# Shared filter sum on ScalarE and GpSimd ahead of the filters, and memory preparation in three split passes, in a decoder trunk

## The chip, the cores and the metric

The kernel runs on one core of a Trainium2 chip. The time is the device time of one execution in microseconds; the profile is of one execution of its own. The core has five engines with a queue each: TensorE (PE; its weight loads are shown apart as PEld), VectorE (DVE), ScalarE (ACT), GpSimd (POOL) and SyncE (SP), which here issues the DMAs. An engine executes its queue in order. SBUF is the on-chip memory of 128 partitions, PSUM the eight banks that matmuls write.

## The reference

A trunk of two layers on x of 1024 tokens by 1024 channels, in float32. Layer 0 mixes tokens with a Conformer convolution, layer 1 with an attention that is not touched here. After the mixer each layer does cross-attention into 256 memory tokens (4 heads of 256) and an MLP with squared ReLU. What matters:

```python
def conformer_conv(h, w_pw1, b_pw1, w_dw, b_dw, ln_g, ln_b, w_pw2, b_pw2):
    u = h @ w_pw1 + b_pw1
    a, gate = jnp.split(u, 2, axis=-1)
    u = a * jax.nn.sigmoid(gate)
    u = lax.conv_general_dilated(u, w_dw[:, None, :], window_strides=(1,),
        padding=[(CONV_WIDTH - 1, 0)], dimension_numbers=("NWC", "WIO", "NWC"),
        feature_group_count=D_MODEL) + b_dw          # 31 taps, each channel for itself
    u = jax.nn.silu(layernorm(u, ln_g, ln_b))
    return u @ w_pw2 + b_pw2

def memory_cross_attention(h, mem_n, w_q, w_k, w_v, w_o):   # mem_n = rmsnorm(mem, norm_memsrc_g)
    q = (h @ w_q).reshape(B, S, MEM_HEADS, MEM_HEAD_DIM)
    k = (mem_n @ w_k).reshape(B, MEM_LEN, MEM_HEADS, MEM_HEAD_DIM)
    v = (mem_n @ w_v).reshape(B, MEM_LEN, MEM_HEADS, MEM_HEAD_DIM)
    s = jnp.einsum("bshd,bmhd->bhsm", q, k) / math.sqrt(MEM_HEAD_DIM)
    p = jax.nn.softmax(s, axis=-1)
    return jnp.einsum("bhsm,bmhd->bshd", p, v).reshape(B, S, D) @ w_o
```

## The kernel before

Channels lie on partitions: x is 8 chunks (NCH) of 128 channels, each in two tiles of 512 tokens (HALF). A float32 product is mostly done in three passes on operands that are split into a high part, rounded to the format float32r, and a low part, the rest: low by high, high by low, high by high (`passes`, L262; `product`, L266). The high part is a copy on ACT, the low part a subtraction on DVE (`split`, L150, and `low`, L147). When `passes` gets a single part on each side it issues one plain float32 matmul, which the profile shows as two records.

The stage of the change is the start: `conv_layer` (L293) with `memory_matrices` (L433) interleaved.

- `conv_layer` loads x, normalizes it into split operands and goes over the 8 chunks. `gated_unit` (L362) computes a chunk's gated value by 2 x 2 products of 8 x 3 passes, ACT's sigmoid (sg, L368) and a multiplication on DVE (u, L370). u holds even and odd tokens apart.
- `convolve` (L386) filters a chunk of 128 channels with 31 taps, all on DVE. It uses the identity that even and odd outputs share a sum over the odd tokens with taps added in pairs (`both`: one instruction, L396, and 15 of L400), to which each half adds a filter of differences: d0 with 16 taps for one half, d1 with 15 for the other (L408). Both halves accumulate in X. The instructions are put in order at compile time; in the trace the taps of the two halves alternate. Then each half is added into `acc` (L354) for the layer norm.
- After the last chunk come the layer norm (`layer_norm`: L310 to L318), then `linear` with the weights pw2, whose outputs L324 adds to x.
- `memory_matrices` is a generator that is advanced a step at a time: four steps a head (K, V, the product of wq with K, the product of V with wo), 4 heads, 2 layers, 32 steps. Four steps are asked for before the filters, two a chunk, and the rest after the last chunk. A step loads two weight tiles of 512 KB (`get`, three tiles) and multiplies in plain float32: 16 products of 256 columns for the first three kinds, 8 of 512 columns for the fourth. Results go to DRAM (mqk, mvo) through the evacuations L483 and L501 on ACT. `mem_attention` reads them afterwards.

PSUM has eight banks: here 4 for the preparation, 2 for the gated unit and pw2, 2 shared ones. Small tiles called "t" (norms, squares and the like) rotate through 4 buffers. `tc.high_priority` moves what it encloses ahead at compile time.

Of the kernel before, what the change touches and what calls it, by code (L numbers as in the profile page):

```python
# [19 lines left out]
P = 128  # L20
# [66 lines left out]
def trunk(ctx, tc, a, out):  # L87
# [98 lines left out]
    def add_squares(acc, ch):  # L186

        sq = nrm.tile([P, HALF], F32, name="sq", tag="t", bufs=4)
        act.activation(sq, ch, AF.Square)
        if acc is None:  # L190
            return sq
        dve.tensor_tensor(acc, acc, sq, op=ALU.add)
        return acc
# [99 lines left out]
    def conv_layer(pm, prep):  # L293
        with tc.tile_pool(name="conv", bufs=2) as cp:
# [43 lines left out]
            acc = [cp.tile([P, HALF], F32, name=f"acc{s}", bufs=1) for s in range(2)]  # L338
            for m in range(NCH):
                if m:  # L340
                    u = padded()
                    for sl in HALVES:
                        gated_unit(pm, cp, m, ahead, hs, u[:, :, PAD // 2 :], sl)
                if m + 1 < NCH:
                    ahead = gate_weights(m + 1)
                for _ in range(2):
                    next(prep, None)

                convolve(cp, m, u, pairs[:, m])
# [36 lines left out]
    def convolve(cp, m, u, sums):  # L386


        n, k = S // 2, TAPS // 2
        even, odd = u[:, 0, :], u[:, 1, :]  # L390
        d0 = cp.tile([P, n + k], F32, name="d0")
        d1 = cp.tile([P, n + k - 1], F32, name="d1")
        dve.tensor_tensor(d0, even[:, : n + k], odd[:, : n + k], op=ALU.subtract)
        dve.tensor_tensor(d1, even[:, 1 : n + k], odd[:, : n + k - 1], op=ALU.subtract)
        both = cp.tile([P, n], F32, name="both")
        dve.tensor_scalar(  # L396
            both, odd[:, :n], sums[:, 0:1], col("dw_b", m), op0=ALU.mult, op1=ALU.add
        )
        for j in range(1, k + 1):
            dve.scalar_tensor_tensor(  # L400
                both, odd[:, j : j + n], sums[:, j : j + 1], both, op0=ALU.mult, op1=ALU.add
            )
        out = [X[:, m, sl] for sl in HALVES]
        for s, d, taps in ((0, d0, k + 1), (1, d1, k)):
            y = both
            for j in range(taps):
                w = col("dw_w", m * TAPS + 2 * j + s)
                dve.scalar_tensor_tensor(  # L408
                    out[s], d[:, j : j + n], w, y, op0=ALU.mult, op1=ALU.add
                )  # L410
                y = out[s]
# [21 lines left out]
    def memory_matrices(pp, pq, layer):  # L433
# [4 lines left out]
        def get(src):  # L438
            raw = pp.tile([P, NCH, P], F32, name="praw", bufs=3)
            nc.sync.dma_start(raw, src)  # L440
            return raw

        mem = pp.tile([P, NCH, MEM], F32, name="mem", bufs=1)
        nc.sync.dma_start(mem, a["memT"])
        if layer == 0:
            r = inverse_rms([mem[:, c, :] for c in range(NCH)], RMS_EPS)
# [3 lines left out]
        for c in range(NCH):  # L450
            act.activation(mem[:, c, :], mem[:, c, :], AF.Copy, scale=col(f"src{layer}", c))
        for h in range(MEM_HEADS):
            kv = []
            for w, n in ((wk, "kt"), (wv, "vt")):
                t = bank(pq).rearrange("p (c m) -> p c m", c=2)
                for c in range(2):
                    x = get(w[2 * h + c])
                    product(t[:, c, :], [((x[:, k, :],), (mem[:, k, :],)) for k in range(NCH)])
                o = pp.tile([P, 2, MEM], F32, name=n, bufs=1)
                if w is wk:  # L460
# [4 lines left out]
                    with tc.high_priority(offset=SMALL_FIRST):  # L465
                        dve.tensor_tensor(o, t, rb, op=ALU.mult)
                else:
                    act.copy(o, t)
                kv.append(o)
                yield  # L470
            kt, vt = kv
            for j in range(2):

                x = get(wq[h, j])
                for g in range(2):
                    t = bank(pq).rearrange("p (f m) -> p f m", f=2)
                    o = pp.tile([P, 4, P], F32, name="o").rearrange("p (f b) n -> p f (b n)", f=2)
                    for f in range(2):
                        product(t[:, f, :], [
                            ((x[:, 4 * c + 2 * g + f, :],), (kt[:, c, :],)) for c in range(2)  # L480
# [7 lines left out]
            for j in range(2):  # L488

                x = get(wo[h, j])  # L490
                for mc in range(2):
# [3 lines left out]
                            (vt[:, c, mc * P : (mc + 1) * P],),  # L495
                            (x[:, 4 * c : 4 * c + 4, :].rearrange("p b n -> p (b n)"),),
# [866 lines left out]
    with prep_pools(4) as pools, banks(2) as pm:  # L1363
        conv_layer(pm, chain(*(memory_matrices(*pools, l) for l in range(2))))
# [81 lines left out]
```

## Time and profile before

| | us |
|---|---|
| median of 3 runs | 2822.05 (2818.59 to 2823.66) |
| profiled execution | 2825.31 |
| its span | 2823.3 |
| until the last output of pw2 begins | 525.5 |

| whole span | busy us | share |
|---|---|---|
| PE | 2740.8 | 97% |
| DVE | 2030.9 | 72% |
| ACT | 1278.3 | 45% |
| POOL | 703.1 | 25% |

The span runs from the first to the last instruction. Busy shares are averages over stages with different limits, so the stage of the change has to be read by itself. In rows of groups the last parts are: output and inputs by the program's names, shapes, count, then busy us and mean ns of one, then the idle time before them and what ended it. In rows of one line or tile, three durations stand as min/median/max in ns, with the first and the last start in us. In rows of the timeline and the chain the first two numbers are start and length in us. All 512-column float32r passes of the kernel overlap in the pipeline, so a record's length is more than its distance to the next.

### The profile page before, as it was taken

The numbers are of one execution on the slowest core, as the hardware profiler recorded it, in microseconds if no ns is written. First come the engines' busy times: TensorE is split into PE (matmuls) and PEld (weight loads), VectorE is DVE, ScalarE is ACT, GpSimd is POOL, SyncE is SP. The second block draws the span as 40 slices with busy tenths as digits, with TensorE's granted clock in tenths as the row PEclk, the third lists the DMA queues.
The fourth block names the chain that finished last, engine by engine and source line by source line (L and its number), as shares of the span: only waits on it lengthen the run. The fifth ranks groups of instructions, "written<-read, shape, count | busy, mean of one in ns | idle before, by whom it ended". The sixth has DMA issues, their size and how long they took to land.

```text
span 2823.3 us, 36214 instructions
## 1 busy us (share of the span) xinstructions
PE 2740.8 (97%) x12968; PEld 2261.3 (80%) x12968; DVE 2030.9 (72%) x3358; ACT 1278.3 (45%) x2293; POOL 703.1 (25%) x473
## 2 busy tenths in 40 slices
PE   8999999999999999999899999989999999989998
PEld 6777777888888877888688888878888788878886
DVE  5999984555776576777788888875546855577776
ACT  5212143433555553333466666673423655543332
POOL 0000000000065625774000000000000365525773
PEclk9999999999999999999899999999999999999999
DMA  6334364322165585652222221243213455655651
GB/s 219 120 119 135 114 206 124 101 90 70 65 230 177 178 309 187 227 199 89 69 68 70 57 65 55 69 136 98 94 64 105 149 176 190 218 208 197 227 201 61
DMA packets 165428, 390.68 MB, mean 138 GB/s; under 512 B 17264, under 2 KB 46192, under 8 KB 164992
## 3 DMA queue, kind: packets, MB, share of 16 engines
q1 hardware_dynamic: 165248, 388.37, 40.9%
q8 instruction: 102, 1.67, 0.2%
q14 instruction: 78, 0.64, 0.1%
HBM read 270.79 MB, written 113.31 MB: 136 GB/s over the span
## 4 chain that ended last, share of the span: by engine, by line
PE 74%; DVE 12%; ACT 5%; DMA 5%; issue 3%; POOL 1%; SPq 0%; DVEq 0%; POOLq 0%; ACTq 0%
PE mm L1070 34%; PE mm L269 29%; PE mm L1255 5%; DVE w L148 2%; DVE op L148 2%; DVE x L408 1%; PE mm L1341 1%; DVE x L1310 1%; DMA ua<-x 1%; ACT x L1315 1%; PE mm L1353 1%; PE mm L1354 1%; DVE both L400 1%; DVE wl L148 1%; ACT pth L151 1%
## 5 line engine op out<-in xcount | busy, mean ns | idle before, releaser
L1070 PE MATMUL mm<-op,w 128*128 128x512 f32 x5424 | 1242.4, 391 | 24.5 <-ACT m L955 8.7
L1070 PEld LDWEIGHTS mm<-op,w 128*128 128x128 f32 x5424 | 1020.5, 189 | 243.2 <-ACT m L955 9.6
L269 PE MATMUL mm<-op,wh 128*128 128x512 f32 x1056 | 330.5, 394 | 4.2 <-DVE op L148 4.2
L148 DVE TENSOR_TENSOR w<-r,w 128x512 fp32r<-128x512 f32 x264 | 262.6, 998 | 30.5 <-ACT w L653 30.5
L653 ACT CAST w<-r 128x512 fp32r<-128x512 f32 x264 | 163.3, 622 | 262.0 <-PE mm L1070 233.2
L269 PEld LDWEIGHTS mm<-op,wh 128*128 128x128 f32 x1056 | 200.2, 190 | 48.5 <-DVE op L148 6.5
L1255 PE MATMUL mm<-op,wh 128*128 128x512 f32 x736 | 231.4, 396 | 0.0
L148 DVE TENSOR_TENSOR w<-t,w 128x512 fp32r<-128x512 f32 x180 | 178.2, 1005 | 63.2 <-ACT w L653 63.1
L269 PE MATMUL mm<-op,wl 128*128 128x512 f32 x528 | 210.5, 400 | 7.1 <-DVE wl L148 6.2
L207 POOL TENSOR_TENSOR r<-v,mhalf 128x4 f32<-128x4 f32 (+1 forms) x15 | 16.8, 1117 | 741.0 <-DVE v L205 741.0
L647 POOL TENSOR_TENSOR t<-r,t 128x512 f32<-128x512 f32 x104 | 174.9, 1681 | 91.4 <-DVE w L148 54.2
L653 ACT CAST w<-t 128x512 fp32r<-128x512 f32 x180 | 112.0, 622 | 169.8 <-PE mm L1070 140.6
L151 ACT CAST wh<-raw 128x1024 fp32r<-128x1024 f32 x96 | 100.7, 1050 | 193.8 <-PE mm L269 97.5
L865 POOL TENSOR_TENSOR x<-x,x 128x512 f32<-128x512 f32 x112 | 160.2, 1455 | 112.6 <-ACT x L878 101.6
L967 DVE TENSOR_TENSOR x<-mm,x 128x512 f32<-128x512 f32 x160 | 109.5, 684 | 91.1 <-PE mm L1070 73.7
L1255 PEld LDWEIGHTS mm<-op,wh 128*128 128x128 f32 x736 | 139.2, 189 | 26.7
L269 PE MATMUL mm<-op,xsh 128*128 128x512 f32 x512 | 158.0, 393 | 0.0
L1255 PE MATMUL mm<-op,wl 128*128 128x512 f32 x368 | 155.0, 421 | 1.9 <-ACT q L1275 1.9
L151 ACT CAST pth<-mm 128x512 fp32r<-128x512 f32 (+1 forms) x224 | 105.9, 495 | 108.5 <-PE mm L556 80.8
L408 DVE SCALAR_TENSOR_TENSOR x<-d,par,x 128x512 f32<-128x512 f32 x232 | 154.5, 746 | 0.0
L647 POOL TENSOR_TENSOR t<-r,r 128x512 f32<-128x512 f32 x52 | 80.2, 1542 | 295.1 <-DMA r<-in_ff_w 191.0
L1315 ACT ACTIVATE x<-x,nb 128x128 f32<-128x128 f32 (+7 forms) x128 | 99.5, 778 | 109.3 <-DVE nb L1313 100.0
(188 smaller groups left out, 4689.6 us busy)
## 6 DMA issues: line engine op xcount, KB each, us to landing
r<-in_ff_w SPq DMA_DIRECT2D x128, 512.0 KB, 4.0
op<-ua SPq DMA_DIRECT2D x80, 512.0 KB, 6.8
us<-x SPq DMA_DIRECT2D x128, 256.0 KB, 2.9
op<-us SPq DMA_DIRECT2D x64, 512.0 KB, 5.6
raw<-mvo SPq DMA_DIRECT2D x32, 512.0 KB, 3.4
ua<-ul SPq DMA_DIRECT2D x64, 256.0 KB, 2.2
ua<-uh SPq DMA_DIRECT2D x60, 256.0 KB, 2.3
raw<-in_pw SPq DMA_DIRECT2D x24, 512.0 KB, 4.7
```

The lines of the kernel that those rows point to most:

```text
L148: dve.tensor_tensor(lo, src, hi.bitcast(F32), op=ALU.subtract)
L151: act.copy(hi, src)
L269: pe.matmul(out_ps, x, y, start=i == 0, stop=i == len(terms) - 1)
L400: dve.scalar_tensor_tensor(both, odd[:, j : j + n], sums[:, j : j + 1], both, op0=ALU.mult, op1=ALU.add)
L408: dve.scalar_tensor_tensor(out[s], d[:, j : j + n], w, y, op0=ALU.mult, op1=ALU.add)
L647: (dve if g in (2, 3, UP, UP + 1) else pool).tensor_tensor(t, raws[g, x], raws[g, y], op=ALU.subtract)
L653: act.copy(highs[n][0], raws[steps[n][:2]])
L865: eng.tensor_tensor(u[g, x], y1, y2, op=op_)
L967: dve.tensor_tensor(v, sums[key], v, op=ALU.add)
L1070: pe.matmul(sums[key], y, z, start=first and i == 0, stop=n == last_of[key] and i == len(terms) - 1, skip_group_check=True,)
L1255: pe.matmul(t, x, y, start=n == 0, stop=n == len(terms) - 1)
L1315: act.activation(x[:, :n], x[:, :n], AF.Exp, bias=nb, accum_out=rs)
```

## The change

1. In the chunk loop, the gated unit of the next chunk and the new `shared_sum` of the next chunk are issued before the filters of the present one; the first chunk's sum is issued before the loop.
2. `shared_sum` computes `both` with ACT forming each product of a tap (one ACTIVATE for each of the 16 pairs of taps, 15 into tiles "t") and POOL adding the 15 products up, in place of DVE.
3. `convolve` accumulates in one PSUM bank (`acc`, a pool of its own) instead of in X; the last tap of each half writes X. The two halves use the same bank. d0 and d1 have one buffer instead of two.
4. Memory preparation works in three split passes. Weights are loaded in halves of 256 KB (`half`, four tiles, which the memory's own loads use as well); ACT copies the high part, POOL subtracts for the low part. The memory itself is split into `memh` (ACT) and `meml` (DVE); K and V results are split with `split` (ACT and DVE). The preparation has 3 PSUM banks instead of 4.

```diff
-    def conv_layer(pm, prep):
+    def conv_layer(pm, pc, prep):
...
+            ready = u, shared_sum(cp, 0, u, pairs[:, 0])
             for m in range(NCH):
-                if m:
-                    u = padded()
-                    for sl in HALVES:
-                        gated_unit(pm, cp, m, ahead, hs, u[:, :, PAD // 2 :], sl)
+                now = ready
                 if m + 1 < NCH:
                     ahead = gate_weights(m + 1)
                 for _ in range(2):
                     next(prep, None)
-                convolve(cp, m, u, pairs[:, m])
+                if m + 1 < NCH:
+                    u = padded()
+                    for sl in HALVES:
+                        gated_unit(pm, cp, m + 1, ahead, hs, u[:, :, PAD // 2 :], sl)
+                    ready = u, shared_sum(cp, m + 1, u, pairs[:, m + 1])
+                convolve(cp, pc, m, *now)
...
+    def shared_sum(cp, m, u, sums):
+        n, k = S // 2, TAPS // 2
+        odd = u[:, 1, :]
+        both = cp.tile([P, n], F32, name="both")
+        act.activation(both, odd[:, :n], AF.Identity, scale=sums[:, 0:1], bias=col("dw_b", m))
+        for j in range(1, k + 1):
+            t = nrm.tile([P, HALF], F32, name="tap", tag="t", bufs=4)
+            act.activation(t, odd[:, j : j + n], AF.Copy, scale=sums[:, j : j + 1])
+            pool.tensor_tensor(both, both, t, op=ALU.add)
+        return both
...
-        both = cp.tile([P, n], F32, name="both")
-        dve.tensor_scalar(
-            both, odd[:, :n], sums[:, 0:1], col("dw_b", m), op0=ALU.mult, op1=ALU.add
-        )
-        for j in range(1, k + 1):
-            dve.scalar_tensor_tensor(
-                both, odd[:, j : j + n], sums[:, j : j + 1], both, op0=ALU.mult, op1=ALU.add
-            )
-        out = [X[:, m, sl] for sl in HALVES]
+        acc = bank(pc)
         for s, d, taps in ((0, d0, k + 1), (1, d1, k)):
             y = both
             for j in range(taps):
+                o = X[:, m, HALVES[s]] if j == taps - 1 else acc
                 w = col("dw_w", m * TAPS + 2 * j + s)
-                dve.scalar_tensor_tensor(
-                    out[s], d[:, j : j + n], w, y, op0=ALU.mult, op1=ALU.add
-                )
-                y = out[s]
+                dve.scalar_tensor_tensor(o, d[:, j : j + n], w, y, op0=ALU.mult, op1=ALU.add)
+                y = acc
...
+        def half(src):
+            raw = pp.tile([P, NCH // 2, P], F32, name="praw", bufs=4)
+            nc.sync.dma_start(raw.rearrange("p k n -> p (k n)"), src.rearrange("p k n -> p (k n)"))
+            return raw
+
         def get(src):
-            raw = pp.tile([P, NCH, P], F32, name="praw", bufs=3)
-            nc.sync.dma_start(raw, src)
-            return raw
+            halves = []
+            for i in range(2):
+                raw = half(src[:, 4 * i : 4 * i + 4, :])
+                hi, lo = (pp.tile([P, NCH // 2, P], F32R, name=f"p{x}", bufs=3) for x in "hl")
+                act.copy(hi, raw)
+                pool.tensor_tensor(lo, raw, hi.bitcast(F32), op=ALU.subtract)
+                halves.append((hi, lo))
+            return halves
...
+        memh, meml = (pp.tile([P, NCH, MEM], F32R, name=f"mem{x}", bufs=1) for x in "hl")
+        sums = None
+        for c in range(NCH):
+            if c % 2 == 0:
+                two = half(a["memT"][:, c : c + 2, :]).rearrange("p (c k) n -> p c (k n)", c=2)
+            ch, g = two[:, c % 2, :], col(f"src{layer}", c)
+            if layer == 0:
+                sums = add_squares(sums, ch)
+            act.activation(memh[:, c, :], ch, AF.Copy, scale=g)
+            dve.scalar_tensor_tensor(
+                meml[:, c, :], ch, g, memh[:, c, :].bitcast(F32), op0=ALU.mult, op1=ALU.subtract
+            )
...
-                    product(t[:, c, :], [((x[:, k, :],), (mem[:, k, :],)) for k in range(NCH)])
-                o = pp.tile([P, 2, MEM], F32, name=n, bufs=1)
+                    product(t[:, c, :], [
+                        ([y[:, k % 4, :] for y in x[k // 4]], (memh[:, k, :], meml[:, k, :])) for k in range(NCH)
+                    ])
+                hi, lo = (pp.tile([P, 2, MEM], F32R, name=n + y, bufs=1) for y in "hl")
...
                         dve.tensor_tensor(o, t, rb, op=ALU.mult)
+                        split(hi, lo, o)
                 else:
-                    act.copy(o, t)
+                    split(hi, lo, t)
...
-    with prep_pools(4) as pools, banks(2) as pm:
+    with prep_pools(3) as pools, banks(2) as pm, banks(1) as pc:
```

27 lines of the change are left out of this document (13 added, 14 removed).

## The prediction

> **What bounds the kernel now.** I read the page first, then busy time by stage, then the groups, waits and chain of the first 525.5 us, the only stage that the diff touches.
>
> ```profile
> span 2823.3 us, 36214 instructions
> PE 2740.8 (97%) x12968; PEld 2261.3 (80%) x12968; DVE 2030.9 (72%) x3358; ACT 1278.3 (45%) x2293; POOL 703.1 (25%) x473
> ```
> ```profile
> L393 DVE TENSOR_TENSOR d<-u x8: 696/704/709, 76.7 to 351.3; 128x527 f32<-128x527 f32 x8
> ```
> ```profile
> L354 DVE TENSOR_TENSOR acc<-acc,x x14: 678/686/695, 150.3 to 388.3; 128x512 f32<-128x512 f32 x14
> ```
> ```profile
> L324 DVE SCALAR_TENSOR_TENSOR x<-mm,par,x x16: 745/751/752, 446.9 to 525.5; 128x512 f32<-128x512 f32 x16
> ```
> ```profile
> core 0: us, PE busy (x) PEld busy (x) DVE busy (x) ACT busy (x) POOL busy (x), PEclk, DMA share, GB/s
> 0.00:76.60 76.60, 63.22 (x252) 48.82 (x253) 40.15 (x68) 38.29 (x69) 3.54 (x11) 0.96 0.61 209
> 76.60:388.90 312.30, 307.75 (x1301) 243.92 (x1299) 306.86 (x442) 63.97 (x107) 0.75 (x6) 1.00 0.43 136
> 388.90:525.50 136.60, 135.72 (x603) 107.83 (x604) 70.63 (x105) 59.34 (x97) 2.01 (x2) 1.00 0.41 125
> ```
>
> Filters run from 76.6 (first difference, L393) to 388.9 (last add into acc, L354); layer norm and pw2 follow until its last output at 525.5 (L324). In the filter stage PE and DVE are both busy 98% of the time; ACT is busy 20%, POOL not at all. DVE sets 312.3/8 = 39.0 us a chunk, and PE fills up with memory preparation. From 388.9 on PE alone is full. The change takes work off both engines, so each has to be priced.
>
> **PE: the three passes.**
>
> ```profile
> 75.74 13.97 PE L269 MATMUL mm<-mem,praw 128*128 128x256 f32 x64
> 57.98 7.03 PE L269 MATMUL mm<-praw,vt 128*128 128x512 f32 x16
> ...
> 575.00 0.28 PE L269 MATMUL mm<-pth,wh 128*128 128x256 f32 x1
> ...
> 576.42 0.28 PE L269 MATMUL mm<-pth,wh 128*128 128x256 f32 x1
> ```
> ```profile
> L269 PE MATMUL mm<-op,wh 128*128 128x512 f32 x256 | 79.0, 391 | 0.0
> L269 PE MATMUL mm<-op,wl 128*128 128x512 f32 x128 | 49.7, 392 | 0.0
> L269 PE MATMUL mm<-praw,vt 128*128 128x512 f32 x32 | 15.4, 599 | 0.0
> L269 PE MATMUL mm<-mem,praw 128*128 128x256 f32 x64 | 14.2, 380 | 0.0
> L269 PE MATMUL mm<-kt,praw 128*128 128x256 f32 x56 | 13.3, 383 | 0.0
> ```
>
> The groups are those of the stage from 388.9 to 525.5. A plain f32 product leaves two records. They start (13.97-0.38)/63 = 0.216 us apart at 256 columns and (7.03-0.60)/15 = 0.43 at 512, so a product takes 0.43 or 0.86 us. Split passes already run elsewhere: at 256 columns, in the memory attention, twelve of them take 576.42-575.00, 0.118 each. At 512 columns it is pw2's pace: PE's full 135.7 us of the last stage less the plain products there, 120 x 0.216 + 32 x 0.43 = 39.7, and some 8 of small ones leave 88 for 384 passes, 0.228 each. Three passes cost 0.355 or 0.684. By the loops there are 2 x 4 x (16+16+16) = 384 products of 256 columns and 2 x 4 x 8 = 64 of 512. Saved: 384 x 0.077 = 29.6 and 64 x 0.176 = 11.3, together 41 us of PE work.
>
> **DVE: the sum leaves, the filter chain changes.**
>
> ```profile
> L408 DVE SCALAR_TENSOR_TENSOR x<-d,par,x 128x512 f32<-128x512 f32 x232 | 154.5, 746 | 0.0
> ```
> ```profile
> 276.77 0.76 DVE both L400
> ...
> 277.56 0.76 DVE both L400
> ...
> 288.33 14.00 DVE x L408 x21
> ```
> ```profile
> L148 DVE TENSOR_TENSOR w<-r,w 128x512 fp32r<-128x512 f32 x264 | 262.6, 998 | 30.5 <-ACT w L653 30.5
> ```
> ```profile
> L148 DVE TENSOR_TENSOR w<-r,w x264: 675/689/1820, 714.9 to 2787.6; 128x512 fp32r<-128x512 f32 x132
> ```
> ```profile
> L967 DVE TENSOR_TENSOR x<-mm,x x160: 674/682/693, 1060.0 to 2807.5; 128x512 f32<-128x512 f32 x160
> ```
>
> - The sum's 16 instructions go: 15 taps 0.785 from start to start (276.77 to 277.56) and a first step a little shorter, -12.3 us a chunk.
> - The 31 filter taps ran two chains in turn, 14.00/21 = 0.667 each. With one PSUM accumulator for both halves they are one dependent chain: 0.785 each, as the sum's was, so 31 x 0.118 = +3.6. No row has DVE writing PSUM. Reading it costs nothing visible (L324 0.751, L408 0.746); the ends are 0.667 (no dependence felt) and 1.0 (the slow L148 group), and I take 0.785, the same operation in a dependent chain.
> - Low parts of kt and vt, 0.69 each as L354, one head in two chunks: +0.7. The memory's own 16 low parts (256 columns, so less than 0.69 each) fall in two lots of 8: the first under DVE's idle time of the start (40 of 76.6 us busy), the second, under 5.5 us or 0.7 a chunk, into the allowance below.
> - POOL now runs beside DVE. In the MLP, where it also does, a subtraction with both inputs in SBUF has a median of 0.689 but reaches 1.82 and means 0.998; an addition with one input in PSUM never exceeds 0.693. Per chunk 8.5 instructions keep two SBUF inputs (d0, d1, two first taps, two acc adds, two wl, half a kt): 8.5 x 0.31 = +2.6. Ends: 0, and a whole POOL operation each, 11.
>
> DVE: 39.0-12.3+3.6+0.7+2.6 = 33.6 us a chunk.
>
> [...]
>
> **POOL and ACT: what they take over.**
>
> ```profile
> L647 POOL TENSOR_TENSOR t<-r,t 128x512 f32<-128x512 f32 x104 | 174.9, 1681 | 91.4 <-DVE w L148 54.2
> ...
> L865 POOL TENSOR_TENSOR x<-x,x 128x512 f32<-128x512 f32 x112 | 160.2, 1455 | 112.6 <-ACT x L878 101.6
> ```
> ```profile
> L647 POOL TENSOR_TENSOR t<-r,r x52: 1286/1301/2285, 789.4 to 2754.4; 128x512 f32<-128x512 f32 x52
> ```
> ```profile
> L501 ACT ACTIVATE o<-mm,mem_r 128x512 f32<-128x512 f32 x20 | 13.7, 687 | 36.7 <-DMA mqk<-o 18.0 <-DMA mvo<-o 15.3 <-PE mm L269 3.4
> ```
>
> POOL gets 15 adds a chunk, and a low part for each 512 columns of memory weights: two steps a chunk, two loads a step, two halves a load, so 8. One costs 1.29 undisturbed, 1.46 (L865) to 1.68 (L647) beside a DVE with more two-input work than this one will have. I take 1.46: 23 x 1.46 = 33.6 a chunk (29.7 to 38.6). ACT gains 16 taps, 8 copies and half a head's split, at L501's 0.69 some 17 us on 64/8 = 8: enough room, though its taps wait for POOL at four shared "t" tiles, with the sigmoids and PSUM evacuations queued behind them.
>
> PE per chunk: gate 96 x 0.228 = 21.9, plus two steps of 16 products, 11.4: 33.3. So DVE, POOL and PE stand within 0.3 us of one another. For handing over I add 0.9 (before, with two engines full, 1.5% or 0.6 was lost): 34.5 us a chunk.
>
> The first sum has nothing ahead of it: 0.69 + 15 x 1.46 = 22 us from 76.6, so the filters start at 98.5. They end at 98.5 + 8 x 34.5 = 374.5, 14 us earlier than 388.9. Issuing the next gate ahead adds nothing by itself: PE already runs ahead of the filters, as its full windows show.
>
> **After the filters.**
>
> ```profile
> 417.89 1.30 DVE L148 TENSOR_TENSOR op<-x,op 128x512 fp32r<-128x512 f32 x2
> ...
> 430.72 3.08 DVE L317 TENSOR_TENSOR x<-x,mm 128x512 f32<-128x512 f32 x5 [2.33 <-PE mm L167]
> ```
>
> Between 388.9 and 525.5 PE was the bound (pw2 87.5, preparation 39.7, small products 8). Less preparation will be left, and layer norm will then show. Its first half's last low parts were done 30 us after the filters (419), and its second half's could not be before 431 + 8 x 1.3 = 441, 52 after; PE has a bank's or two's worth of first-half products, 5 to 11 us, in between. As one chain now ends the first half's sum 12 us ahead of the second's, I take 36 us, then 87.5: the last output at 374.5 + 123.5 = 498. Ends: 30 and 47. PE check: 7 gates (153), 28 of the 32 preparation steps (28/32 of 384 x 0.355 + 64 x 0.684 = 180, so 157) and 8 of small products are 318 in the 334 from 76.6 to 410.5. So 525.5 - 498 = 27.5 us are won.
>
> **Loads and the start.**
>
> ```profile
> praw<-in_mem_wk SPq DMA_DIRECT2D x16, 512.0 KB, 4.8
> ```
> ```profile
> L440 SPq DMA_DIRECT2D praw<-in_mem_wk x16: 327/380/1361, 1.6 to 399.7; - x16
> ```
>
> The bytes stay; the loads double, 64 to 128 issues (plus 8 for the memory) on SP's queue, where x, gate weights and stores stand behind a load that waits for one of the four tiles. An issue takes 0.33 to 0.38 us, some 24 us more over 450, and nothing on PE waits unless a tile is late. A half is split 2 us before PE needs it; two halves ahead cover that, else each wait costs up to a landing, 4.8. At the start PE saves 6 us on its first steps but waits for a copy, a low part and for x behind the memory's halves; I take 0 (-6 to +6, a landing and a POOL operation). The other 2298 us are unchanged.
>
> The profiled execution took 2825.31 us, its span 2823.3; 2825.3 - 27.5 = 2798. The median of the runs is 3.3 lower: **2795 us**.
>
> **Rivals.**
>
> 1. PE alone is the bound: the whole 41 us come off, 2781. For it: PE 98% busy in both stages. Against it: 22 us of first sum and layer norm stand in the chain. 0.14.
> 2. The chain through PSUM costs more: 0.90 a tap adds 3.6 a chunk, so all of the gain, 2822; half of that gives 2809. Nothing in the trace excludes it. [...] With POOL a little slow it makes the small-gain case, 2809 to 2822: 0.19.
> 3. Slower: POOL sets the pace, and ACT, held at its four tiles, passes it on to PE. At 525.5 the filters may end at 402: (402-98.5)/8 = 37.9 a chunk, 1.65 us a POOL operation. L647's 1.68 is past that; at 1.82 (41.9 a chunk) the filters end at 433.5, +31, 2853. For it: 1.68 was measured. Against it: there DVE had far more two-input work. [...] 0.14.
>
> The forecast (2784 to 2809) has 0.53. Measurement tells 0.2%, 5.6 us: the forecast, rival 1 and the upper part of rival 2's gains are faster, 0.77; within it half of rival 2, 0.10; slower 0.13. The range 2779 to 2824 leaves out rival 3 and the far ends.
>
> **What would show it.** Right: filter taps 0.79 apart, POOL 1.4 to 1.5 an operation and 85 to 95% busy, chunks 33 to 36 apart, filters ending near 375, last pw2 output near 498. Wrong: taps over 0.85; POOL over 1.65; ACT sigmoids waiting for POOL; PE waiting for a split or a load; gate 0 ending after 82; a first scores stage that does not move with pw2.

## The result and the profile after

The changed kernel takes 2984.06 us (median; 2977.40 to 2987.57) against 2822.86 for the kernel before on the same chip: a ratio of 1.057 (1.055 to 1.059), 161 us slower. The forecast was 2795. The profiled execution took 2985.76 us. First its span and busy times, from the page:

```profile
span 2983.5 us, 37938 instructions
PE 2747.1 (92%) x13416; PEld 2295.7 (77%) x13416; DVE 2008.1 (67%) x3262; ACT 1444.1 (48%) x2557; POOL 1036.2 (35%) x721
```

The span is 160 us longer, and PE, the engine that was to be relieved, is busy for as long as before (2740.8). So it waits more, and some of what it does takes longer: after a wait of 8.0 us, passes of 256 columns start 0.21 us apart (from 344.6 to 347.4), and 0.12 apart further on. The marks of the stages are the rows of the first difference d0, of the adds into `acc` and of pw2's outputs (their first and last starts), then the busy times between these marks:

```profile
L410 DVE TENSOR_TENSOR d<-u x8: 703/1169/1564, 84.8 to 422.5; 128x527 f32<-128x527 f32 x8
```
```profile
L358 DVE TENSOR_TENSOR acc<-acc,x x14: 680/832/1779, 170.0 to 480.2; 128x512 f32<-128x512 f32 x14
```
```profile
L324 DVE SCALAR_TENSOR_TENSOR x<-mm,par,x x16: 746/751/752, 582.7 to 675.2; 128x512 f32<-128x512 f32 x16
```
```profile
core 0: us, PE busy (x) PEld busy (x) DVE busy (x) ACT busy (x) POOL busy (x), PEclk, DMA share, GB/s
0.00:84.70 84.70, 60.23 (x312) 52.13 (x313) 51.40 (x78) 48.73 (x89) 31.54 (x30) 0.92 0.57 190
84.70:481.00 396.30, 282.81 (x1450) 240.61 (x1448) 275.44 (x342) 191.22 (x305) 260.77 (x198) 0.85 0.29 92
481.00:600.00 119.00, 90.10 (x512) 75.85 (x513) 41.55 (x65) 68.19 (x118) 48.88 (x39) 0.84 0.44 135
600.00:676.00 76.00, 75.39 (x333) 62.10 (x331) 28.25 (x36) 18.78 (x26) 0.00 (x0) 1.00 0.32 93
```

In the filter stage (84.7 to 481) no engine is full: PE 71%, DVE 70%, POOL 66%, ACT 48%. The chunks stand 48.2 us apart ((422.5-84.8)/7) with 33 to 35 us of work in each of the three busiest engines. The last pw2 output starts at 675.2 instead of 525.5: 8 of these 150 us are there when the filters begin, 92 when they end, and 58 more come after them. The last 10 us of the 160 arise in the stages behind, which the change does not touch; no run takes these apart.

Who waited for whom in the filter stage (engine, line and output, what it waited for: us in all, times, longest):

```profile
DVE mm L418 <- POOL both L402: 91.0, 8, 18.8
POOL both L402 <- ACT tap L401: 80.4, 7, 14.7
...
PE mm L269 <- POOL pl L458: 63.9, 17, 14.0
ACT tap L401 <- POOL both L402: 56.4, 82, 1.1
...
PE mm L269 <- ACT o L516: 40.6, 4, 17.5
```

Every engine waits for another: DVE for the sum, POOL for ACT's taps, PE for POOL's low parts and for ACT to evacuate a PSUM bank. So the links form a ring. One turn of it in the timeline of this kernel, of POOL and then of DVE:

```profile
327.53 21.33 POOL L402 TENSOR_TENSOR both<-both,tap 128x512 f32<-128x512 f32 x15 [13.84 <-ACT tap L401]
...
375.36 10.30 POOL L402 TENSOR_TENSOR both<-both,tap 128x512 f32<-128x512 f32 x7 [3.94 <-ACT tap L401]
```
```profile
348.90 1.80 DVE L418 SCALAR_TENSOR_TENSOR mm<-d,par,both 128x512 f32<-128x512 f32 x1 [10.62 <-POOL both L402]
...
373.07 0.75 DVE L374 SCALAR_TENSOR_TENSOR u<-mm,par,sg 128x512 f32<-128x512 f32 x1
```

A chunk's sum runs from 327.5 to 348.9, and there the chunk's first tap starts. The second half of the next gate (u) stands in DVE's queue behind 21 of the 31 taps, at 373.1, and the next sum starts at 375.4. That is 47.8 us a turn, 21.4 of them the sum. Neither the list nor the timeline says which link can be loosened; the runs below try them.

The single operations are as long as forecast, or shorter: the low parts, the additions of the sum, the taps (groups of the page: busy us and mean ns), and passes of 512 columns, which start 0.23 us apart (at 596; the granted clock from 560 to 600 is 1.00).

```profile
L458 POOL TENSOR_TENSOR pl<-praw,ph 128x512 fp32r<-128x512 f32 x128 | 173.6, 1374 | 122.7 <-ACT ph L457 109.0
...
L402 POOL TENSOR_TENSOR both<-both,tap 128x512 f32<-128x512 f32 x120 | 161.2, 1344 | 89.2 <-ACT tap L401 80.4
...
L418 DVE SCALAR_TENSOR_TENSOR mm<-d,par,mm 128x512 f32<-128x512 f32 x216 | 162.8, 754 | 5.2
```
```profile
596.33 0.39 PE L269 MATMUL mm<-pl,vth 128*128 128x512 f32 x1
596.56 0.40 PE L269 MATMUL mm<-ph,vth 128*128 128x512 f32 x1
596.79 0.39 PE L269 MATMUL mm<-ph,vtl 128*128 128x512 f32 x1
```

### The profile page after: what moved, and what is told of

The parts are those of the page before. It is cut to its first block, busy times and chain, and to the rows that moved or that the text cites. A ratio compares the mean times of both kernels' runs of the same rounds, so it can differ in the third digit from the quotient of the medians.

```text
span 2983.5 us, 37938 instructions
## 1 busy us (share of the span) xinstructions
PE 2747.1 (92%) x13416; PEld 2295.7 (77%) x13416; DVE 2008.1 (67%) x3262; ACT 1444.1 (48%) x2557; POOL 1036.2 (35%) x721
## 4 chain that ended last, share of the span: by engine, by line
PE 60%; DVE 9%; ACT 5%; issue 5%; DMA 4%; POOL 1%; SPq 0%; DVEq 0%; POOLq 0%; ACTq 0%
PE mm L1103 32%; PE mm L269 17%; PE mm L1288 5%; DVE op L148 2%; DVE w L148 1%; PE mm L1374 1%; DVE x L1343 1%; ACT x L1348 1%; POOL pl L458 1%; PE mm L1386 1%; PE mm L1387 1%; ACT pth L151 1%; DMA r<-in_ff_w 1%; PE mm L1338 1%; PE mm L1339 1%
## 5 line engine op out<-in xcount | busy, mean ns | idle before, releaser
L458 POOL TENSOR_TENSOR pl<-praw,ph 128x512 fp32r<-128x512 f32 x128 | 173.6, 1374 | 122.7 <-ACT ph L457 109.0
L269 PE MATMUL mm<-op,wl 128*128 128x512 f32 x528 | 208.8, 397 | 7.2 <-DVE wl L148 4.6
L402 POOL TENSOR_TENSOR both<-both,tap 128x512 f32<-128x512 f32 x120 | 161.2, 1344 | 89.2 <-ACT tap L401 80.4
L418 DVE SCALAR_TENSOR_TENSOR mm<-d,par,mm 128x512 f32<-128x512 f32 x216 | 162.8, 754 | 5.2
```

The costliest lines, as they stand in the source:

```text
L269: pe.matmul(out_ps, x, y, start=i == 0, stop=i == len(terms) - 1)
L402: pool.tensor_tensor(both, both, t, op=ALU.add)
L418: dve.scalar_tensor_tensor(o, d[:, j : j + n], w, y, op0=ALU.mult, op1=ALU.add)
L458: pool.tensor_tensor(lo, raw, hi.bitcast(F32), op=ALU.subtract)
```

## The experiments

The expectations stand as they were recorded, with the theories as they were then. Times are medians, each ratio is to the kernel before on the same chip.

### Each part alone

The moved gate and sum with PSUM taps, and `memory_matrices` as before:

```diff
 # the changed kernel, with the function of the kernel before
-    def memory_matrices(pp, pq, layer):   # three passes
+    def memory_matrices(pp, pq, layer):   # plain float32
```

> The changed kernel with the memory preparation as it was before (plain float32, whole loads, no split), and everything else of the change. Theory A (block): the sum stands as one uninterrupted block on ACT (15 taps, each waiting for POOL) and on POOL; PSUM evacuations and the sigmoid queue behind the taps, PE stops, and the next gate comes late. Most of the loss in the filter stage stays: chunks 44 to 48 us apart, total 2880 to 2930. Theory B (POOL overloaded by 23 operations a chunk): with 15 left, chunks 33 to 37 apart, total 2790 to 2815. Theory C (the split preparation is slow by itself: load, copy, low part and product in a chain with few tiles): as B, 2790 to 2825.

Measured: 2936.05 us, 1.040 (1.039 to 1.042). The moved sum alone costs 114 us, somewhat more than theory A has; the chunks stand 47 us apart, as in that theory.

The split preparation alone, in the kernel before (sum and taps as before, one buffer for d0 and d1 so that it fits):

```diff
 # the kernel before, with the function of the changed kernel
-    def memory_matrices(pp, pq, layer):   # plain float32
+    def memory_matrices(pp, pq, layer):   # three passes
```

> The kernel before with the split memory preparation alone (low parts on POOL, half loads, four load tiles; four PSUM banks; one buffer for d0 and d1). Theory A: no block; DVE sets 39 to 41 us a chunk as before, PE has slack, filters end at 390 to 405, total 2805 to 2835. Theory B: POOL has only 8 operations a chunk: the same. Theory C: the preparation holds up PE by itself, in the filter stage and above all after it, where 58 us were lost: total 2860 to 2900.

Measured: 3012.26 us, 1.067 (1.066 to 1.069): 190 us more, above the range of every theory. The two costs don't add up (161 together), and the row of POOL's low parts says why; the first is this kernel's, the second that of the changed one:

```profile
L450 POOL TENSOR_TENSOR pl<-praw,ph x128: 1255/1297/16597, 12.8 to 629.4; 128x512 fp32r<-128x512 f32 x128
```
```profile
L458 POOL TENSOR_TENSOR pl<-praw,ph x128: 1255/1293/2702, 12.2 to 596.7; 128x512 fp32r<-128x512 f32 x128
```

The median is the same, but single low parts last up to 16.6 us. The timeline of DVE and of POOL at one of them:

```profile
320.71 1.42 DVE L408 SCALAR_TENSOR_TENSOR x<-d,par,both 128x512 f32<-128x512 f32 x2
322.05 15.99 DVE L408 SCALAR_TENSOR_TENSOR x<-d,par,x 128x512 f32<-128x512 f32 x24
```
```profile
325.67 13.48 POOL L450 TENSOR_TENSOR pl<-praw,ph 128x512 fp32r<-128x512 f32 x1 [4.81 <-ACT ph L449]
```

DVE runs 24 taps without a gap (15.99/24 = 0.67 apart, both inputs in SBUF), and POOL's operation, begun at 325.7, ends at 339.2, 1.1 us after the last of them. In the changed kernel, whose third part is the PSUM accumulator, none lasts over 2.7 us.

### The sum: who adds, who holds, who is first

Four variations of the changed kernel that each relieve one engine. Low parts of the weights on DVE (0.69 us each) instead of POOL:

```diff
-                pool.tensor_tensor(lo, raw, hi.bitcast(F32), op=ALU.subtract)
+                low(lo, raw, hi)
```

> The changed kernel with the low parts of the memory weights on DVE (0.69 each) in place of POOL, which keeps only the sum. Theory A: the block on ACT and its hold on PSUM evacuations stay: chunks 44 to 49 apart, total 2930 to 2980. Theory B: POOL is relieved, chunks 36 to 40, total below 2850. Theory C with the low part on POOL as the slow link: below 2880.

Measured: 2965.28 us, 1.051 (1.049 to 1.053), 19 below the changed kernel. POOL has the sum alone here, and still the chunks stand 47.7 us apart. DVE has 8 x 0.69 = 5.5 us more a chunk, so this run alone does not clear POOL; the moved sum with the plain preparation, with 15 operations a chunk and 47 us, points the same way.

The sum on DVE again, but still ahead of the filters:

```diff
-        act.activation(both, odd[:, :n], AF.Identity, scale=sums[:, 0:1], bias=col("dw_b", m))
+        dve.tensor_scalar(both, odd[:, :n], sums[:, 0:1], col("dw_b", m), op0=ALU.mult, op1=ALU.add)
...
-            act.activation(t, odd[:, j : j + n], AF.Copy, scale=sums[:, j : j + 1])
-            pool.tensor_tensor(both, both, t, op=ALU.add)
+            dve.scalar_tensor_tensor(
+                both, odd[:, j : j + n], sums[:, j : j + 1], both, op0=ALU.mult, op1=ALU.add
+            )
```

> The changed kernel with the sum's instructions on DVE as before (a first step and 15 taps), still issued ahead of the filters, with one PSUM accumulator and the split preparation. Theory A: no block on ACT and POOL; DVE has 39 + 3.6 (one chain) + 2 to 4 (sharing with POOL) = 44 to 47 a chunk; PE is not held; what is lost after the filters stays in part; total 2860 to 2920. Theory C: as the changed kernel, 2940 or more. The difference to e2 is the cost of the one chain and of the order.

Measured: 2965.14 us, 1.050 (1.049 to 1.052). Neither ACT nor POOL has the sum, and the chunks stand 48.6 us apart: now DVE is full, 361 of 375 us (its filter stage: PE, PEld, DVE, ACT, POOL in turn).

```profile
88.00:463.00 375.00, 279.60 (x1423) 234.35 (x1421) 361.01 (x467) 103.23 (x172) 112.46 (x77) 0.88 0.31 97
```

Every second tap of the sum on DVE, the others on ACT and POOL:

```diff
+            if j % 2:   # as in the change
...
+            else:
+                dve.scalar_tensor_tensor(
+                    both, odd[:, j : j + n], sums[:, j : j + 1], both, op0=ALU.mult, op1=ALU.add
+                )
```

> The changed kernel with the sum's 8 odd taps on ACT and POOL and its 7 even ones on DVE. Theory A (length of the block): the block is 22 us minus 7 x 1.4 plus 7 x 0.8, some 17 us, and ACT is held half as long, but DVE's queue has 5.5 us more a chunk and every second tap is a hand-over between POOL and DVE: 44 to 48 a chunk, total 2930 to 2970. If the load of POOL were the cause, 40 or less and below 2900.

Measured: 2978.38 us, 1.057 (1.055 to 1.059); 6 below the changed kernel, and the chunks are 48.6 us apart: no difference that counts.

A chunk's first tap put behind the evacuation of the next chunk's whole gate in DVE's order:

```diff
+                if after is not None and s == j == 0:
+                    # order only, no semaphore: first tap after u of the next gate's second half
+                    tc.add_manual_dep(i, after.name, ...)
```

> The changed kernel with one order more on DVE: the first tap of a chunk's filters stands behind the evacuation of the next chunk's second gate half. In the changed kernel that tap waits for the shared sum on POOL, and the gate's evacuations stand behind it. Theory A1 (DVE's queue closes the circle sum, filters, gate, sum): gate and sum come off the circle, chunks 36 to 43 apart instead of 49, total 2890 to 2950. Theory A2 (ACT's block of waiting taps alone holds PE): chunks still 47 to 50, total 2970 to 3000.

Measured: 2993.75 us, 1.062 (1.059 to 1.065). Held back like this, DVE waits 43.5 us for the gate's products (u, L375), which PE has behind preparation passes that wait for low parts (55.1 us). The gate itself came no earlier; the chunks stand 49.5 us apart.

Then the same question without the split preparation. First the hold of ACT: its taps get ten tiles of their own (the moved sum alone, otherwise as above).

```diff
-            t = nrm.tile([P, HALF], F32, name="tap", tag="t", bufs=4)
+            t = cp.tile([P, HALF], F32, name="tap", bufs=10)
```

> The moved gate and shared sum alone (plain preparation), with ten tiles of their own for ScalarE's scaled taps in place of the four shared ones. Theory H (hold: ScalarE's taps wait for GpSimd through the four tiles, and the evacuations and sigmoids of the next chunk wait behind them): the 56 us of waits of ScalarE's taps for GpSimd fall below 25, the chunks come below 45 us apart from 47, and the whole is under 2910, against 2936. Theory C (circle: the sum of a chunk is started only when the gate of the chunk is there, and the first tap waits for the whole sum's 21 us whichever way ScalarE is held): ScalarE's waits fall and the chunks stay 46 to 48 us apart, 2925 to 2940.

Measured: 2933.83 us, 1.040 (1.036 to 1.043), against 2936.05. The hold is gone and nothing is gained. First the kernel with four tiles, then the one with ten:

```profile
DVE mm L418 <- POOL both L402: 120.7, 8, 17.4
...
ACT tap L401 <- POOL both L402: 56.0, 80, 1.1
```
```profile
DVE mm L418 <- POOL both L402: 120.7, 8, 17.4
...
PE mm L269 <- DVE u L374: 53.0, 7, 9.2
...
ACT tap L401 <- POOL both L402: 0.3, 1, 0.3
```

ACT's waits fall from 56.0 to 0.3 us, DVE's stay at 120.7. One round of the ring in the timeline of this kernel, of DVE and then of POOL:

```profile
236.19 0.76 DVE L418 SCALAR_TENSOR_TENSOR mm<-d,par,both 128x512 f32<-128x512 f32 x1 [14.62 <-POOL both L402]
...
249.51 0.75 DVE L374 SCALAR_TENSOR_TENSOR u<-mm,par,sg 128x512 f32<-128x512 f32 x1
...
259.42 0.75 DVE L374 SCALAR_TENSOR_TENSOR u<-mm,par,sg 128x512 f32<-128x512 f32 x1
```
```profile
214.80 21.35 POOL L402 TENSOR_TENSOR both<-both,tap 128x512 f32<-128x512 f32 x15 [25.50 <-ACT tap L401]
...
261.71 1.38 POOL L402 TENSOR_TENSOR both<-both,tap 128x512 f32<-128x512 f32 x1 [25.50 <-ACT tap L401]
```

The sum of a chunk runs until 236.1, and at 236.2 the chunk's first tap starts. In DVE's queue the two halves of the next gate (u) stand behind 17 and behind 27 of the 31 taps, so the second half leaves at 259.4, and only then can the next sum start, at 261.7. One round is 236.2-214.8 = 21.4 of sum and 261.7-236.2 = 25.5 of taps and what stands among them: 46.9 us. The sum was moved ahead in the program, but in the queues it is not ahead.

The last step of this line raises the next gate and its sum in the compile-time order (ten tiles kept):

```diff
+                    with tc.high_priority(offset=SMALL_FIRST):
+                        # gated_unit(m + 1) and shared_sum(m + 1), as they are
```

> The moved gate and shared sum alone (plain preparation, ten tap tiles), with the next chunk's gate and sum raised in the compile-time order, so that VectorE's queue has the second half of the next gate behind some 5 to 12 of a chunk's 31 taps instead of behind 26. Theory R (ring by order: the sum starts only when VectorE, late in a chunk's taps, evacuates the next gate, and the next chunk's first tap then waits for most of the sum's 21 us): the wait of VectorE's first tap for the sum falls from 15 us a chunk below 5, the chunks stand 39 to 42 us apart instead of 46.8, and the whole is 2850 to 2895 against 2934. Theory P (PSUM: it is TensorE's banks, held by ScalarE's late evacuations, that make the gate late): the gate's products are late whatever VectorE's order, 2915 to 2940.

Measured: 2872.28 us, 1.018 (1.016 to 1.020): 62 us from an order alone. Its waits for the sum, its differences and its stages:

```profile
DVE mm L419 <- POOL both L403: 15.2, 2, 14.0
```
```profile
L411 DVE TENSOR_TENSOR d<-u x8: 699/925/1797, 78.8 to 332.4; 128x527 f32<-128x527 f32 x8
```
```profile
78.00:381.00 303.00, 264.93 (x1092) 208.33 (x1091) 261.97 (x326) 136.08 (x218) 171.46 (x126) 0.95 0.32 101
381.00:496.00 115.00, 110.36 (x452) 81.64 (x451) 34.27 (x57) 51.05 (x88) 2.02 (x2) 0.99 0.60 189
```

DVE's wait falls from 120.7 to 15.2. The gates' two halves now stand together behind the first tap of a chunk (at 287.2, for one), and the chunks stand (332.4-78.8)/7 = 36.2 us apart, less than expected; the filters end at 381, eight before the kernel before. But the whole is still 50 us slower: what the filters gained, PE did not get. It idles 38 us in the filter stage, and 359 of the 896 records of preparation passes start after the last add into acc, against 152 in the kernel before. They are done between 381 and 496, with PE full.

### The preparation: order, halves, low parts

The low part of the weights is left out, so POOL has no work; the high part takes its place in the passes (split preparation alone, otherwise as above). That nearly doubles the products, which the expectation calls less exact: of this kernel only the times are of use.

```diff
-                hi, lo = (pp.tile([P, NCH // 2, P], F32R, name=f"p{x}", bufs=3) for x in "hl")
+                hi = pp.tile([P, NCH // 2, P], F32R, name="ph", bufs=3)
...
-                pool.tensor_tensor(lo, raw, hi.bitcast(F32), op=ALU.subtract)
-                halves.append((hi, lo))
+                halves.append((hi, hi))
```

> The split preparation alone in the kernel before, as in the run of the preparation alone, but with the low part of the weights left out: all three passes take the high part (same passes, same copies on ACT, same half loads; the values of the preparation are less exact). Theory C1 (the low part on POOL and its waits are the cost): total 2800 to 2825, PE waits little. Theory C2 (a product now waits for ACT's copy in ACT's queue, with few tiles, and POOL matters little): total 2900 or more.

Measured: 2895.84 us, 1.027 (1.026 to 1.029). That is just short of theory C2's range, and 116 of the 190 us are gone: POOL's part, its waits included. The filters end at 394, some 5 us later than in the kernel before; the rest of the loss comes after them. What PE waits for from 390 on, and how busy it is:

```profile
PE mm L158 <- DVE acc L354: 49.3, 1, 49.3
PE mm L269 <- ACT kth L151: 16.9, 1, 16.9
```
```profile
390.00:460.00 70.00, 36.47 (x165) 32.00 (x166) 44.59 (x74) 37.38 (x63) 2.01 (x2) 0.61 0.07 23
```

A small product of the layer norm's mean stands at the head of PE's queue for 49 us, with preparation passes behind it. The compile-time order could not place them before: the scaled K^T (`kt`) now takes one of the four "t" tiles, which the layer norm uses too, so the preparation has to follow it. The weights loaded in halves, in plain float32 in the kernel before, cost a little by themselves:

```diff
-            raw = pp.tile([P, NCH, P], F32, name="praw", bufs=3)
...
+            for i in range(2):
+                raw = pp.tile([P, NCH // 2, P], F32, name="praw", bufs=4)
...
```

> The kernel before with the weights of the preparation loaded in halves of 256 KB into four tiles (instead of whole ones of 512 KB into three), still plain float32. If the loads and the smaller depth are a cost: PE waits for praw, total 2830 to 2850. If not: 2820 to 2826.

Measured: 2835.16 us, 1.005 (1.004 to 1.007): 14 us above the kernel before on its chip (2821.48). In the filter stage PE waits 6.0 us for the loads; where the others arise was not looked into.

A buffer of its own for `kt`, in three kernels: the one with high parts alone, the split preparation alone, and the changed kernel.

```diff
-                        o = nrm.tile([P, HALF], F32, name="kt", tag="t", bufs=4)
-                        o = o.rearrange("p (c m) -> p c m", c=2)
+                        o = pp.tile([P, 2, MEM], F32, name="kt", bufs=1)
```

> The preparation in three passes with ScalarE's high copy alone (the low part of the weights is left out, so all three passes take the high part), on the kernel before, with a buffer of its own for the scaled K^T. Theory O: the preparation ends beside the filters as in the kernel before, and the 50 us in which TensorE waited for the layer norm's mean are gone: 2815 to 2840, against 2896 with the shared tile. Theory S (the copies and the four tiles alone keep the passes late): 2880 to 2900.

> The preparation in split passes alone, on the kernel before, with a buffer of its own for the scaled K^T. Theory O: the layer norm's token means no longer stand at the head of TensorE's queue while passes wait behind them; 50 to 70 us below the same kernel with the shared tile, about 2945 to 2960, and GpSimd's low parts still take up to 16 us beside the uninterrupted taps. Theory S: within 10 us of the same kernel with the shared tile, 3000 to 3020.

> The changed kernel, with one tile changed: the scaled K^T of the memory preparation gets a buffer of its own in place of one of the four that rotate among it, the filters' taps and the layer norm's temporaries. Theory O (order: the shared tile ties the preparation to the layer norm, so that a good third of its passes is left behind the filters): the wait of TensorE for ScalarE's scaled K^T after the filters (16.9 us) goes, and the whole is 20 to 50 us below the changed kernel, 2935 to 2965. Theory S (speed: the copy, low part and product of each piece are too slow whatever the order): the same passes are late, within 10 us of the changed kernel, 2975 to 2995.

Measured: 2846.59 us, 1.009 (1.006 to 1.011); 2984.49, 1.057 (1.055 to 1.060); 2966.97, 1.051 (1.049 to 1.054). In the first the wait for the mean falls from 49.3 to 9.8 us, and 49 us are won, a little less than theory O has. In the others it is 28 and 17, also less than expected: there the passes are late for other reasons as well.

The other reason of the second is taken away by the taps: into a PSUM bank as in the change, the sum where it was, `kt` with its own buffer.

```diff
-        out = [X[:, m, sl] for sl in HALVES]
+        acc = bank(pc)
...
+                o = X[:, m, HALVES[s]] if j == taps - 1 else acc
```

> The preparation in split passes alone (K^T in its own buffer), the shared sum where it was in the kernel before, but the 31 taps accumulate in a PSUM bank as in the change (the preparation then has three banks instead of four). Theory V (VectorE's back-to-back operations on two inputs of the shared memory shut GpSimd out): the low parts of 13 to 16 us are gone but for those beside the 16 operations of the sum, which stay on two such inputs (about 11 us each at most), GpSimd's mean falls from 2.0 below 1.7 us, and the whole is 2890 to 2940, against 2984. If the chain of load, copy, low part and product through four tiles is what costs the time, the whole stays above 2960.

Measured: 2904.88 us, 1.029 (1.028 to 1.031). That is 80 us less once the taps no longer shut POOL out, net of what the dependent chain costs DVE. POOL's low parts and the filter stage:

```profile
L449 POOL TENSOR_TENSOR pl<-praw,ph x128: 1264/1477/2370, 12.6 to 492.8; 128x512 fp32r<-128x512 f32 x128
```
```profile
85.00:467.00 382.00, 331.52 (x1813) 279.22 (x1811) 360.87 (x475) 141.57 (x247) 161.01 (x114) 0.95 0.42 132
```

No low part is over 2.4 us. What is left is DVE at 361 of 382 us: the taps as one dependent chain, and the low parts of memory, K and V, are more than it had to spare. By these runs the preparation in three passes needs DVE relieved, and the moved sum needs an order that relieves it. The next run has both.

### Both orders mended in the whole change

```diff
+                    with tc.high_priority(offset=SMALL_FIRST):   # gate and sum of m + 1
...
+                        o = pp.tile([P, 2, MEM], F32, name="kt", bufs=1)
```

> The changed kernel with both orders mended: the scaled K^T in a buffer of its own, and the next chunk's gate and sum raised in the compile-time order. Theory R: the chunks come from 48 to 40 to 43 us apart and the whole is 2890 to 2930, against 2967 with the buffer alone. If GpSimd's low parts or ScalarE's taps held at four tiles set the pace instead, the chunks stay at 46 to 49 and the whole within 12 us of 2967.

Measured (own buffer for `kt`, next gate and sum raised): 2962.87 us, 1.050 (1.048 to 1.052), only 4 below the buffer alone. What gave 62 us with the plain preparation gives next to nothing with the split one. The order itself took effect, as DVE's waits in the filter stage show:

```profile
DVE wl L148 <- ACT wh L151: 21.4, 6, 7.4
...
DVE mm L419 <- POOL both L403: 14.0, 1, 14.0
```

The wait for the sum is 14.0 us, against 98.2 with the buffer alone. But the chunks come only from 47.8 to (401.6-88.0)/7 = 44.8 us apart, between the two expectations, because other waits have taken its place in DVE's queue: for ACT's copies of the gate's weights (21.4) and of V (16.3), for the gate's sigmoids (18.9), and for the products of the gate (12.6) and of K (10.6). Two more kernels take away the low parts of the weights (left out, as above), and then the hold of ACT as well:

```diff
-                pool.tensor_tensor(lo, raw, hi.bitcast(F32), op=ALU.subtract)
+                lo = hi
...
+            if j % 2:   # the second kernel alone
+                t = cp.tile([P, HALF], F32, name="tap", bufs=3)
+            else:
                 t = nrm.tile([P, HALF], F32, name="tap", tag="t", bufs=4)
```

> The change with both orders mended (scaled K^T in its own buffer, next gate and sum raised), and the low part of the weights left out: all three passes take the high part, and GpSimd has the sum alone. If GpSimd's low parts between load and product are what keeps the mended change at 2963, the whole falls to 2800 to 2850. If ScalarE's taps, held at four tiles by the sum, are (54 us of TensorE's waits are for the sigmoid behind them), it stays above 2880.

> The same (the low part of the weights is left out), with seven tiles for ScalarE's taps, three of their own beside the four shared ones. If the hold of ScalarE at four tiles counts once the order is mended, TensorE's waits for the sigmoid fall from 54 us below 25 and the whole is 25 us or more below the same kernel with four. If not, both are within 10 us.

Measured: 2916.65 us, 1.034 (1.032 to 1.036), and 2896.72, 1.027 (1.024 to 1.029). PE's waits in the filter stage of the three, in this order:

```profile
PE mm L269 <- ACT sg L373: 53.0, 6, 14.3
...
PE mm L269 <- POOL pl L459: 29.9, 20, 15.7
```
```profile
PE mm L269 <- ACT sg L373: 50.0, 6, 11.1
...
PE mm L269 <- ACT ph L458: 19.0, 5, 13.3
```
```profile
PE mm L269 <- ACT sg L373: 33.2, 6, 9.6
...
PE mm L269 <- ACT ph L461: 18.9, 4, 12.8
```

The low parts are worth 46 us and three more tiles 20, which lies between the two cases expected for them; the expectations named one or the other as the cause, and it is both in part. Without low parts PE waits for ACT's copies (ph) instead. With the order mended, PE waits for the sigmoid that stands behind ACT's taps, the hold that counted for nothing in the plain preparation before its order was mended. Even so 75 us to the kernel before stay. How they divide among ACT's copies, the remaining hold and passes left over (409 of 1344 records behind the filters) was not settled. No version that ran beats the kernel before.

## Why the prediction was wrong

The step that failed is the one from work to time: "DVE, POOL and PE stand within 0.3 us of one another. For handing over I add 0.9". The chunks came 48.2 us apart, not 34.5. The 0.9 was taken from a stage in which PE and DVE were both full and each stood idle for about 5 of 312 us. The change makes a ring through the queues of four engines: a gate's product on PE, its evacuation on ACT and DVE, the sum on ACT and POOL, the taps on DVE. A ring's time is the sum along it, not the fullest engine's share: 47.8 us a turn in this kernel's trace, with 33 to 35 us of work on each of the three busiest engines. What the ring costs was shown with the plain preparation. In the whole change no single mend frees it, and how its 161 us divide stays open in part. Of the prediction's own signs of being wrong two came plainly: PE waited for splits, and gate 0 ended after 82, at 84.8.

- **"Issuing the next gate ahead adds nothing by itself"** was the sentence that hid it. The full windows showed that PE runs ahead, not where u stands in DVE's queue. In the kernel before it made no difference that u came late in a chunk, since DVE did everything in turn. With the sum elsewhere its place puts most of the sum's 21 us on DVE's path, 15 us of waiting a chunk with the plain preparation (120.7 over 8 chunks), and moving it won 62 us there. In the whole change the same move brought the wait from 98.2 to 14.0 us and won 4: DVE waited for ACT and PE instead.
- **PE's three passes.** Their price was right (0.23 apart at 512 columns). "Nothing on PE waits unless a tile is late" was not: 63.9 us of waits for low parts and 40.6 for evacuations in the filter stage. Of the preparation's 1344 records 408 were left after the last add, 30%, where 4 steps of 32 were forecast to be left at the layer norm.
- **POOL.** 1.46 us was too high (1.344 and 1.374), so by the reckoning all should have been well. The 0 for "loads and the start" was also off: gate 0 ended 8 us late, and halves alone cost 14.
- **DVE.** The tap in PSUM was right: 0.79 from start to start (the 14 from 236.98 of the kernel with ten tiles, 11.05 us in all), where 0.785 was forecast and rival 2 had 0.90. That it keeps POOL from being shut out was worth 80 us in the split preparation alone; the text counted it as a cost.
- **First sum.** 22 us forecast, though its terms 0.69 + 15 x 1.46 make 22.6; from the sum's first step at 84.9 to the first tap at 107.1 it was 22.2. That it fits so well is luck in part, for POOL was faster than forecast.
- **After the filters.** 123.5 us forecast, 194.3 measured (480.9 to 675.2). "Layer norm will then show" was right in kind. But `kt`'s move into the "t" tiles, in the diff for all to see, was not priced: it tied the order of the preparation to the layer norm. In the run with high parts alone this was 49 us, in the whole change 17. By the prediction's own prices the 408 passes left behind are an estimated 56 us of PE work (336 x 0.118 and 72 x 0.228) where it had 22.5, so some 34 of the missing 71 us come from them; what is left beside these two was not taken apart.
- **Rival 3** named the hold of ACT at four tiles and the right sign, but let it decide from 1.65 us a POOL operation. POOL stayed far below, and the hold alone was worth 2 us (plain preparation, order as in the change) and, in part, 20 (order mended, no low parts, three more tiles). So it was not the main mechanism either. No rival spoke of order.

## What to carry to other kernels

When work moves from one engine's stream to others, draw the ring it closes and add up the times along it, with each link's place in its queue; balanced shares do not give the time of a ring. Look where in the queue the instruction stands that starts the moved work, not only where the program has it. And a tile that moves into a shared rotating buffer ties the compile-time order of both its users: count that as a dependence.

## What the runs showed of the hardware

DVE's taps on two SBUF inputs, issued without a gap from two chains (0.67 apart), made single POOL subtractions last 13.5 to 16.6 us (the split preparation alone), where 1.3 is the median; as one dependent chain in PSUM they let them through in 1.3 to 2.4 (the split preparation with PSUM taps). In that run the sum's taps still read two SBUF inputs, each waiting for the one before, and no low part beside them was longer than that 2.4 either. In the split preparation alone 13 such taps of the sum ran from 139.4 to 155.1, 15.65/13 = 1.20 us each, and the six low parts that began in that time took about 1.6 us each (1.67 + 4.88 + 3.13 = 9.7 us). So in these runs two SBUF inputs alone did not shut POOL out; whether the gap or the PSUM operand frees the filter taps, no run separates. In the timeline of the split preparation alone, POOL's operation of 13.48 us did not get through when the DVE instruction of 0.75 us running at its start ended: some 18 of them started after POOL's operation had.

PE's granted clock was lower where PE was less busy. It was 1.00 at 98% (the filter stage before), 0.95 at 87% (order mended, plain preparation; taps in PSUM), 0.85 at 71% (changed kernel) and 0.61 at 52% (high parts alone, 390 to 460). The share does not settle it alone: the first 84.7 us of the changed kernel had 0.92, also at 71%. Where the clock was low, passes were longer: in the changed kernel PE waited 8.0 us for an evacuation on ACT, then its passes of 256 columns took 0.41 us and started 0.21 apart (344.6 to 347.4, clock 0.50), and further on 0.28 us and 0.12 apart (347.5 to 355, clock 1.00). So idle time of PE went with longer passes in what it still did. That this keeps PE's busy time where it was, though 41 us of work were reckoned off it, is argued and not shown.
